# Loads ahead of the last reads, 31 tiles ahead, four last rounds by block: a hybrid retention and PEER layer on one core

## The chip, the cores and the metric

One core of a Trainium2 chip runs the whole layer. The metric is the device time of the program in microseconds (us). The engines are TensorE (PE in the profile, PEld its weight loads), VectorE (DVE), ScalarE (ACT), GpSimd (POOL) and SyncE (SP, which here only issues transfers); each works through its own instructions in order and waits on semaphores for the others. DMA transfers are issued from the queues of SP, ACT and POOL.

## The reference

512 latent tokens and 256 context tokens of width 1024, one layer, fp32. Cut to what matters here:

```python
mod = silu(c) @ ada_w + ada_b                  # six rows of 1024: sh1, sc1, g1, sh2, sc2, g2
lg = log_sigmoid(ret_decay)                    # 2 x 4 decays
proj = modulate(rmsnorm(x), sh1, sc1) @ w_in   # pooling mixer, retention q k v, gates
x = x + g1 * (merged @ w_out)                  # merged: gated sum of pooling and retention
hf = modulate(rmsnorm(x), sh2, sc2)
# PEER: 8 heads; product keys give 16 of 16384 experts to each token and head
q = hf @ wq;  s1, s2 = q . keys;  top 16 of each;  top 16 of the sums -> eidx, g = softmax
act = gelu(u[eidx] . hf)
x = x + g2 * sum over experts (g * act) * v[eidx]
out = rmsnorm(x) * final_g
```

## The kernel before

fp32 products are made of three passes (`mm3`, L151 to L153): every operand is split into a part `hi` rounded to the engine's format (`split_hi`, a cast on ScalarE) and the remainder `lo` (`split_lo`, L168, a subtraction on VectorE or, where the caller says so, GpSimd). A weight tile is loaded from DRAM into one of three `raw` buffers (`load`, L158); the buffer comes free when hi and lo have been made.

**Front.** `mods` computes the modulation vectors from 512 KB pieces of ada_w (VectorE reductions, L292) and makes the first weight groups' low parts on GpSimd. `attention` starts with 31 operations on 128x8 numbers that turn the decays into `lg`, and ends with the pooling and retention branches. `post` multiplies by w_out, adds the gated residual, normalises each block of 128 tokens (`normed`: TensorE multiplies by a diagonal matrix, which gives the transposed block, `ht` is that scaled and shifted, `hfT` its split). `row_bcast` (L199) turns one modulation vector into a tile with that vector in all 128 partitions by 16 TensorE matmuls; it is called four times, for g1, a2, s2 and, near the end, g2.

**Experts.** The tokens of block 0 take their experts one by one: 128 gathers (`fetch`, L983, a gather of u and v rows), a dot product (L991), a gelu and a combine (L1002). The other three blocks (384 tokens) take all 16384 experts densely, as 128 tiles of 128 experts: `up` (24 matmuls and a gelu) gives `a`; it is multiplied by `G`, the routing weights in dense form (`run_times`, L1145), split into ph and pl (`weigh`), and `down` adds its product with the tile's v rows into Y (18 matmuls for the three blocks).

The dense G is made in 24 rounds, the hot phase: VectorE makes one-hot matrices of 16 tokens (`onehots`), TensorE multiplies them (L1087), ScalarE moves the product into `st` (L1088), which is stored to DRAM (`gd`). G is read back in pieces of 8 tiles (`read`). In this phase up tiles are already made in halves (`run_up`), up to `AHEAD` of them, with loads `ask`ed three tiles ahead and splits made by `prep`. `tick` lets one step of the routes (`topk`) of block 0 run, interleaved with other work.

The main loop over 128 rounds j: weigh the next tile, split its v rows, load u tiles, read a part of a piece of G, `down`, dots of arrived gathers, `run_times`, combines, lows of u, up of a later tile, sometimes a tick, new gathers from round `GATHER` on. After round `LATE` the rows for the last normalisation are loaded and block 0 is finished. The last two rounds run block by block, so that each block's `finish` (scale, residual, norm, store) can start when its Y is complete.

The order on every engine is the order in which the code above is written, except where stated: no scheduler moves instructions inside the expert part, whose schedule is manual.

## Time and profile before

| | before |
|---|---|
| runs | 1816.27, 1817.89, 1818.47 us, median 1817.89 |
| profiled execution | 1820.35 us, its span 1818.6 us |
| PE busy | 1733.3 us, 95% of the span, 9913 matmuls |
| DVE / ACT / POOL busy | 1348.6 / 774.6 / 442.8 us |
| granted TensorE clock, mean | 0.988 of full speed |
| DMA | 404 MB, mean 222 GB/s |

The span is from the first to the last instruction of the profiled execution; some 1.75 us of its time lie outside it. Busy time of PE counts instructions in flight, which overlap. In a timeline row an idle time in brackets is the time for which the engine did nothing just before that instruction, with the operation whose completion ended it. A row with x2 or more joins instructions of one form that follow each other.

### The profile page before, as it was taken

To read this page: it belongs to the slowest core of one execution; us is meant where nothing else is said; L and a number is where in the kernel's file an instruction comes from. 1 tells how busy PE (TensorE), PEld (TensorE's weight loads), DVE (VectorE), ACT (ScalarE), POOL (GpSimd) and SP (SyncE) were. 2 spreads that over 40 slices of the span, in tenths; PEclk is the share of its full clock that TensorE was granted. 3 is DMA by queue.
4 is the path that set the end of the run, shared out by engine and by line. 5 is a ranking of instruction groups with operands and counts; after the bars stand their busy time and mean duration, and the time that the engine had idled before them with its cause. 6 is when DMAs were issued, how large, how long until landed. Compare 5 with 4: busy or idle time off the path is not lost.

```text
span 1818.6 us, 26049 instructions
## 1 busy us (share of the span) xinstructions
PE 1733.3 (95%) x9913; PEld 1556.5 (86%) x9913; DVE 1348.6 (74%) x2402; ACT 774.6 (43%) x1304; POOL 442.8 (24%) x403
## 2 busy tenths in 40 slices
PE   7999999999989989896999999999999999999996
PEld 4889988888989988885888888889999999999995
DVE  6866365663559999987958777887888778887766
ACT  6343245222344348872334434344444444444443
POOL 2222220001047730005622222222222222222200
PEclk9999999999999999997999999999999999999998
DMA  7311133674242226773478888889898898889852
GB/s 305 108 47 47 59 122 128 231 253 153 70 150 67 87 81 243 266 270 102 139 299 300 294 325 318 296 319 328 328 330 301 327 329 313 328 309 335 309 172 95
DMA packets 133550, 404.02 MB, mean 222 GB/s; under 512 B 10800, under 2 KB 60208, under 8 KB 113840
## 3 DMA queue, kind: packets, MB, share of 16 engines
q1 hardware_dynamic: 111104, 241.39, 39.3%
q0 software_dynamic: 18432, 134.23, 19.0%
q10 hardware_dynamic: 3888, 26.74, 3.6%
q8 instruction: 77, 1.26, 0.3%
q14 instruction: 49, 0.40, 0.1%
HBM read 372.95 MB, written 29.36 MB: 221 GB/s over the span
## 4 chain that ended last, share of the span: by engine, by line
PE 46%; DVE 7%; ACT 5%; DMA 3%; issue 2%; POOL 1%; ACTq 0%; DVEq 0%; POOLq 0%
PE Y L152 8%; PE Y L153 8%; PE Y L151 8%; PE ps L153 7%; PE ps L151 7%; PE ps L152 7%; ACT st L1088 3%; DMA raw<-uvd 2%; DVE lo L168 1%; DVE o L1075 1%; ACT hi L163 1%; DMA gd<-st 1%; DVE eq L1072 1%; DVE uv L991 1%; POOL lo L168 0%
## 5 line engine op out<-in xcount | busy, mean ns | idle before, releaser
L163 ACT CAST hi<-raw 128x1024 fp32r<-128x1024 f32 x332 | 343.6, 1050 | 232.9 <-DMA raw<-uvd 150.8
L168 DVE TENSOR_TENSOR lo<-raw,hi 128x1024 fp32r<-128x1024 f32 x285 | 364.1, 1279 | 102.7 <-ACT hi L163 100.9
L153 PE MATMUL ps<-hfT,lo 128*128 128x384 f32 x1120 | 378.5, 338 | 16.9 <-DVE lo L168 16.9
L151 PE MATMUL ps<-hfT,hi 128*128 128x384 f32 x1120 | 380.6, 340 | 8.1 <-ACT a L1110 7.6
L152 PE MATMUL ps<-hfT,hi 128*128 128x384 f32 x1120 | 376.8, 336 | 1.3 <-POOL hfT L146 1.3
L983 POOL DMA_INDIRECT uv<-uv,eidx x128 | 196.8, 1537 | 604.1 <-DVE acc L1002 572.5
L151 PE MATMUL Y<-hi,ph 128*128 128x512 f32 x768 | 301.0, 392 | 10.1 <-ACT a L1110 8.4
L152 PE MATMUL Y<-lo,ph 128*128 128x512 f32 x768 | 302.9, 394 | 6.4 <-POOL lo L168 5.8
L153 PE MATMUL Y<-hi,pl 128*128 128x512 f32 x768 | 302.6, 394 | 0.0
L153 PEld LDWEIGHTS ps<-hfT,lo 128*128 128x128 f32 x1120 | 211.3, 189 | 21.8 <-DVE lo L168 21.8
L151 PEld LDWEIGHTS ps<-hfT,hi 128*128 128x128 f32 x1120 | 211.5, 189 | 13.7 <-ACT a L1110 8.3
L152 PEld LDWEIGHTS ps<-hfT,hi 128*128 128x128 f32 x1120 | 211.6, 189 | 5.6 <-POOL hfT L146 1.8
L1002 DVE SCALAR_TENSOR_TENSOR acc<-uv,act,acc 128x1024 f32<-128x1024 f32 x127 | 163.0, 1283 | 29.1 <-ACT act L994 17.5
L151 PEld LDWEIGHTS Y<-hi,ph 128*128 128x128 f32 x768 | 145.4, 189 | 39.0 <-ACT a L1110 8.7
L152 PEld LDWEIGHTS Y<-lo,ph 128*128 128x128 f32 x768 | 145.2, 189 | 37.2 <-POOL lo L168 7.8
L1110 ACT ACTIVATE a<-ps 128x384 f32<-128x384 f32 x128 | 62.6, 491 | 259.9 <-PE ps L153 253.8
L153 PEld LDWEIGHTS Y<-hi,pl 128*128 128x128 f32 x768 | 145.1, 189 | 30.7 <-DVE pl L146 0.3
L168 POOL TENSOR_TENSOR lo<-raw,hi 128x1024 fp32r<-128x1024 f32 x47 | 119.7, 2554 | 182.5 <-ACT hi L163 182.5
L146 DVE TENSOR_TENSOR pl<-a,ph 128x384 fp32r<-128x384 f32 x128 | 73.1, 571 | 118.1 <-ACT ph L145 118.0
L991 DVE SCALAR_TENSOR_TENSOR uv<-uv,hf 128x1024 f32<-128x1024 f32 x128 | 154.4, 1219 | 0.0
L1088 ACT ACTIVATE st<-ps 128x512 f32<-128x512 f32 x96 | 91.0, 1109 | 13.2 <-DMA gd<-st 7.1
L993 ACT ACTIVATE act<-act 128x1 f32<-128x1 f32 x128 | 25.9, 202 | 162.2 <-DVE uv L991 162.2
(287 smaller groups left out, 2912.4 us busy)
## 6 DMA issues: line engine op xcount, KB each, us to landing
raw<-uvd SPq DMA_DIRECT2D x252, 512.0 KB, 6.0
ada<-ada SPq DMA_DIRECT2D x48, 512.0 KB, 5.4
gd<-st ACTq DMA_DIRECT2D x24, 1024.0 KB, 5.6
raw<-w_in SPq DMA_DIRECT2D x44, 512.0 KB, 4.2
G<-gd SPq DMA_DIRECT2D x85, 256.0 KB, 7.6
raw<-wq SPq DMA_DIRECT2D x16, 512.0 KB, 4.1
raw<-ret_out SPq DMA_DIRECT2D x8, 512.0 KB, 4.8
raw<-w_out SPq DMA_DIRECT2D x8, 512.0 KB, 3.6
```

The costliest lines, as they stand in the source:

```text
L146: (eng_lo or nc.vector).tensor_tensor(lo, src, hi.bitcast(F32), ALU.subtract)
L151: mm(out, a[0], b[0], start=first, stop=False)
L152: mm(out, a[0], b[1], start=False, stop=False)
L153: mm(out, a[1], b[0], start=False, stop=last)
L163: self.nc.scalar.copy(hi, raw)
L168: eng.tensor_tensor(lo, raw, hi.bitcast(F32), ALU.subtract)
L983: self.nc.gpsimd.indirect_dma_start(out=t, out_offset=None, in_=self.I["uv"], in_offset=bass.IndirectOffsetOnAxis(ap=self.eidx[:, s:s + 1] ...
L991: nc.vector.scalar_tensor_tensor(t[:, :D], t[:, :D], 1.0, self.hf, ALU.mult, ALU.mult, accum_out=act[:, 0:1])
L993: nc.scalar.activation(act[:, 1:2], act[:, 0:1], AF.Gelu)
L1002: nc.vector.scalar_tensor_tensor(self.acc, t[:, D:], act[:, 1:2], self.acc, ALU.mult, ALU.add)
L1088: nc.scalar.mul(st[:, :, t:t + 4].rearrange("p m t -> p t m"), ps, 1.0 / GSCALE)
L1110: nc.scalar.activation(a, ps[:, :N], AF.Gelu)
```

## The change

AHEAD 30 to 31, LATE 117 to 118, GATHER 9 to 10, and a new LAST = 4. The decay arithmetic moves out of `attention` into `decays`, called at the start of `build` with the same operations. Of the diff, cut:

```diff
+            self.md = dr.tile([4, D], F32, name="md")
...
             nc.sync.dma_start(self.cols, I["cols"])
+            self.decays(hp)
...
-                            w[g].append(self.split_w(self.load(I["w_in"][g][:, 4 * i:4 * i + 4]), nc.gpsimd))
+                            w[g].append(self.split_w(self.load(I["w_in"][g][:, 4 * i:4 * i + 4]), nc.vector))
...
+    def mod_row(self, out, v):
+
+        self.nc.sync.dma_start(out, self.md[v:v + 1].to_broadcast([P, D]))
...
         g1 = p.tile([P, D], F32, name="g1")
-        self.row_bcast(g1, self.modc[:, 0:8])
+        a2 = p.tile([P, D], F32, name="a2")
+        s2 = p.tile([P, D], F32, name="s2")
+        ps = self.ps()
+        nc.tensor.transpose(ps[0:32, 0:P], self.modc, self.ident)
+        rows = p.tile([32, P], F32, name="mrows")
+        nc.scalar.copy(rows, ps[0:32, 0:P])
+        nc.sync.dma_start(self.md.rearrange("v (k p) -> (v k) p", p=P), rows)
+        for row, v in ((g1, 0), (a2, 2), (s2, 1)):
+            self.mod_row(row, v)
...
-                    nc.vector.tensor_scalar(t[:, i], ps[:, i * P:(i + 1) * P], cols[:, 16 + k:17 + k],
-                                            cols[:, 8 + k:9 + k], ALU.mult, ALU.add)
+                    m, c = cols[:, 16 + k:17 + k], cols[:, 8 + k:9 + k]
+                    if i % 2:
+                        nc.scalar.activation(t[:, i], ps[:, i * P:(i + 1) * P], AF.Identity, scale=m, bias=c)
+                    else:
+                        nc.vector.tensor_scalar(t[:, i], ps[:, i * P:(i + 1) * P], m, c, ALU.mult, ALU.add)
                 d = [a[:, 4 * h:4 * h + 4, (b - 1) * P:b * P] for a in hT]
-                self.split(t, d[0], d[1], None, nc.gpsimd)
+                self.split(t, d[0], d[1])
...
-        a2 = p.tile([P, D], F32, name="a2")
-        s2 = p.tile([P, D], F32, name="s2")
-        self.row_bcast(a2, self.modc[:, 16:24])
-        self.row_bcast(s2, self.modc[:, 8:16])
...
-        self.run_up(4)
-        self.prep(QU + 4, nc.vector)
+        self.run_up(5)
...
-            ph = dp.tile([P, N], F32R, name="ph", tag="ph", bufs=2)
-            pl = dp.tile([P, N], F32R, name="pl", tag="pl", bufs=2)
+            if j < P - LAST:
+                ph, pl = [dp.tile([P, N], F32R, name=x, tag=x, bufs=2) for x in ("ph", "pl")]
+            else:
+                ph, pl = [self.ring.tile([P, N], F32R, name=x, tag="a", bufs=AHEAD + 1) for x in ("ph", "pl")]
...
-                self.run_up(2 if i % 3 == 2 else 1)
+                self.run_up(2 if i % 3 == 0 else 1)
...
         self.rt_es.close()
-        read(0, 18, 22)
-        read(0, 22)
+        k = self.split_to
+        self.prep(k, nc.vector)
+        self.prep(k + 1, nc.vector)
         for n in range(2):
             vs[n] = load_v(n)
         nv[1] = 2
+        read(0, 18, 22)
+        read(0, 22)
         self.dp = dp = self.pool("dense")
         place(1)
-        read(1)
-        k = len(self.acts)
-        self.prep(k + 2, nc.vector)
-        self.prep(k + 3, nc.vector)
         tick()
         tick()
         self.run_up(3)
-        self.prep(k + 4, nc.vector)
+        self.prep(k + 2, nc.vector)
...
-            run_v(min(P, j + 4 if deep else j + 2), nc.gpsimd if j + 1 < GATHER else nc.vector)
+            run_v(min(P, j + 4 if deep else j + 2), nc.vector)
...
+            if j < 2:
+                read(1, 12 * j, 12 * j + 12)
...
-            if j < P - 2:
+            if j < P - LAST:
...
+            for n in hi:
+                us[n] = self.split_lo(us[n], hi[n], nc.vector)
+                ns += 1
             for s, act in zip(ready, cr):
                 self.combine(s, slots.pop(s), act)
             done = asked[0]
-            for n in hi:
-                us[n] = self.split_lo(us[n], hi[n], nc.vector)
-                ns += 1
...
-            if j % 4 < 3:
+            if j % 10 in (0, 1, 3, 4, 6, 7, 9):
                 tick()
...
-                self.row_bcast(fin[0], self.modc[:, 24:32])
+                self.mod_row(fin[0], 3)
...
-            for j in (P - 2, P - 1):
+            for j in range(P - LAST, P):
...
-        for b in (0, 0, 1, 2, 1, 3, 1, 2, 3, 3, 2):
+        for b in (0, 0, 1, 1, 1, 2, 2, 2, 3, 3, 3):
```

The lines of the expert part are 21 higher in the changed kernel (L1145 becomes L1166).

The SyncE queue at the end of the hot phase, before. raw_8055 to raw_8262 are u tiles, G_6616 is piece 0 of G (its blocks 10 to 18, 18 to 22, 22 to 24), raw_8327 and raw_8329 are v rows of tiles 0 and 1, G_8334 is piece 1, raw_8336 the last u tile made ahead (29).

```order
L158 DMA raw_8055<-uvd 128x1024
L1124 DMA G_6616<-gd_58 128x8x128
L158 DMA raw_8187<-uvd 128x1024
L158 DMA raw_8262<-uvd 128x1024
L1124 DMA G_6616<-gd_58 128x4x128
L1124 DMA G_6616<-gd_58 128x2x128
L158 DMA raw_8327<-uvd 128x1024
L158 DMA raw_8329<-uvd 128x1024
L1124 DMA G_8334<-gd_58 128x24x128
L158 DMA raw_8336<-uvd 128x1024
```

The same place of the queue with the change: raw_8111 to raw_8318 are u tiles 27 to 30, raw_8324 and raw_8326 the v rows of tiles 0 and 1, G_6603 is piece 0 and G_8333 piece 1.

```order
L1145 DMA G_6603<-gd_59 128x8x128
L159 DMA raw_8111<-uvd 128x1024
L159 DMA raw_8193<-uvd 128x1024
L159 DMA raw_8312<-uvd 128x1024
L159 DMA raw_8318<-uvd 128x1024
L159 DMA raw_8324<-uvd 128x1024
L159 DMA raw_8326<-uvd 128x1024
L1145 DMA G_6603<-gd_59 128x4x128
L1145 DMA G_6603<-gd_59 128x2x128
L159 DMA raw_8668<-uvd 128x1024
L159 DMA raw_8674<-uvd 128x1024
L1145 DMA G_8333<-gd_59 128x12x128
```

Two u tiles and both v tiles now stand ahead of the last two reads of piece 0, and piece 1 is read in two halves further on.

VectorE where the first `a` is multiplied by G, before: the end of a tick's searches (s, sv, si), the three products, pl of tile 0, then the next step of the routes (e).

```order
L922 MATCH_REPLACE s_4759<-sv_8529,s_4759 128x128 x2
L917 MAX sv_8529<-s_4759 128x8 x2
L919 MAX_INDEX si_8530<-sv_8529,s_4759 128x8 x2
L1145 TENSOR_TENSOR a<-a,G 128x384 x3
L146 TENSOR_TENSOR pl<-a,ph 128x384
L967 TENSOR_REDUCE e_8605<-oe 128x16
```

With the change, where lo is the low part of u tile 30:

```order
L943 MATCH_REPLACE s_4732<-sv_8516,s_4732 128x128 x2
L938 MAX sv_8516<-s_4732 128x8 x2
L940 MAX_INDEX si_8517<-sv_8516,s_4732 128x8 x2
L1166 TENSOR_TENSOR a<-a,G 128x384 x3
L147 TENSOR_TENSOR pl<-a,ph 128x384
L169 TENSOR_TENSOR lo<-raw,hi 128x1024
L988 TENSOR_REDUCE e_8610<-oe 128x16
```

The ticks still stand ahead of the products, and the low part of tile 30 comes behind both.

VectorE in a round of the main loop with two gathered rows, before (lo behind pl is that of v, lo at the end that of u; L991 the dots, L1002 the combines):

```order
L146 TENSOR_TENSOR pl<-a,ph 128x384
L168 TENSOR_TENSOR lo<-raw,hi 128x1024
L991 SCALAR_TENSOR_TENSOR uv,act<-uv,hf 128x1024 x2
L1145 TENSOR_TENSOR a<-a,G 128x384
L1002 SCALAR_TENSOR_TENSOR acc<-uv,act,acc 128x1024 x2
L168 TENSOR_TENSOR lo<-raw,hi 128x1024
```

With the change (L1012 the dots, L1023 the combines):

```order
L147 TENSOR_TENSOR pl<-a,ph 128x384
L169 TENSOR_TENSOR lo<-raw,hi 128x1024
L1012 SCALAR_TENSOR_TENSOR uv,act<-uv,hf 128x1024 x2
L1166 TENSOR_TENSOR a<-a,G 128x384
L169 TENSOR_TENSOR lo<-raw,hi 128x1024
L1023 SCALAR_TENSOR_TENSOR acc<-uv,act,acc 128x1024 x2
```

The low part of u has moved ahead of the combines.

## Rows read from the trace of the kernel before

**Rows 1.** Busy time by stretch: us, busy us (instructions) by engine, PEclk, DMA share, GB/s

```profile
844.00:857.00 13.00, 11.09 (x30) 8.34 (x30) 12.43 (x43) 3.63 (x5) 9.13 (x16) 0.65 0.21 72
1150.00:1740.00 590.00, 590.00 (x2947) 532.40 (x2946) 471.37 (x583) 249.68 (x474) 140.67 (x91) 1.00 0.87 318
```

**Rows 2.** Timeline of PE: start us, us, instruction, tiles, [idle before <-releaser]

```profile
70.92 0.39 PE L151 MATMUL ps<-hi,hc 128*128 128x256 f32 x1 [2.54 <-DVE k L146]
...
507.38 0.61 PE L667 MATMUL ps<-diag,xr 128*128 128x128 f32 x4
...
518.84 0.44 PE L152 MATMUL ps<-hfT,hi 128*128 128x384 f32 x1 [1.30 <-POOL hfT L146]
...
808.12 0.33 PE L153 MATMUL ps<-hfT,lo 128*128 128x384 f32 x1
...
812.28 0.34 PE L153 MATMUL ps<-hfT,lo 128*128 128x384 f32 x1
...
828.84 0.69 PE L151 MATMUL ps<-hfT,hi 128*128 128x384 f32 x1 [7.16 <-ACT a L1110]
...
843.59 0.79 PE L151 MATMUL Y<-hi,ph 128*128 128x512 f32 x1 [8.42 <-ACT a L1110]
...
873.76 0.50 PE L152 MATMUL Y<-lo,ph 128*128 128x512 f32 x1 [1.82 <-POOL lo L168]
...
884.14 0.50 PE L152 MATMUL Y<-lo,ph 128*128 128x512 f32 x1 [1.81 <-POOL lo L168]
...
1027.41 0.44 PE L153 MATMUL ps<-hfT,lo 128*128 128x384 f32 x1 [1.13 <-DVE lo L168]
...
1748.59 1.95 PE L199 MATMUL ps<-ident,modc 128*128 128x128 f32 x16
...
1789.46 0.50 PE L151 MATMUL Y<-hi,ph 128*128 128x512 f32 x1 [1.71 <-ACT ph L145]
...
1805.87 0.39 PE L153 MATMUL Y<-hi,pl 128*128 128x512 f32 x1
```

**Rows 3.** Timeline of DVE in the front

```profile
22.43 1.22 DVE L292 SCALAR_TENSOR_TENSOR junk<-ada,crow 128x1024 f32<-128x1024 f32 x1
...
24.05 2.90 DVE L292 SCALAR_TENSOR_TENSOR junk<-ada,crow 128x1024 f32<-128x1024 f32 x1 [0.39 <-DMA ada<-ada]
```

**Rows 4.** Timeline of POOL: the normed blocks, and the first rounds

```profile
516.49 4.54 POOL L146 TENSOR_TENSOR hfT<-ht,hfT 128x512 fp32r<-128x512 f32 x2 [2.70 <-ACT hfT L145]
...
850.25 2.67 POOL L168 TENSOR_TENSOR lo<-raw,hi 128x1024 fp32r<-128x1024 f32 x1
```

**Rows 5.** Timeline of DVE in the hot phase

```profile
689.22 1.22 DVE L1072 TENSOR_TENSOR eq<-ioh,ig 128x2048 f16<-128x2048 f16 x1
...
693.76 1.22 DVE L168 TENSOR_TENSOR lo<-raw,hi 128x1024 fp32r<-128x1024 f32 x1
```

**Rows 6.** Timeline of SP's queue at the end of the hot phase

```profile
804.50 9.97 SPq L1124 DMA_DIRECT2D G<-gd  x2
...
816.47 20.76 SPq L158 DMA_DIRECT2D raw<-uvd  x3
```

**Rows 7.** Timeline of ACT at the last tile made ahead

```profile
827.35 1.04 ACT L163 CAST hi<-raw 128x1024 fp32r<-128x1024 f32 x1 [13.94 <-DMA raw<-uvd]
```

**Rows 8.** Timeline of DVE from the last low parts on, and its last passes

```profile
814.01 0.48 DVE L917 MAX8 sv<-s 128x8 f32<-128x128 f32 x2
...
818.49 0.29 DVE L919 FIND_INDEX8 si<-sv,s 128x8 uint32<-128x128 f32 x1
...
829.57 0.21 DVE L917 MAX8 bv<-cs 128x8 f32<-128x54 f32 x1
...
841.69 1.47 DVE L1145 TENSOR_TENSOR a<-a,G 128x384 f32<-128x384 f32 x3
...
850.62 3.38 DVE L168 TENSOR_TENSOR lo<-raw,hi 128x1024 fp32r<-128x1024 f32 x1
...
1812.59 2.74 DVE L1019 SCALAR_TENSOR_TENSOR od<-od,ss,uv 128x512 f32<-128x512 f32 x4
```

More of the change, by code (lines that the diff above doesn't have):

```diff
@@ L39 @@
 NH = 2
-AHEAD = 30
+AHEAD = 31
 JE = 121
-LATE = 117
-GATHER = 9
+LATE = 118
+LAST = 4
+GATHER = 10
 LAG = 2
@@ L240, in front, with decays @@
                 self.post(op, hx, ys)
+    def decays(self, hp):
+        nc, I = self.nc, self.I
+        dc = hp.tile([P, 8], F32, name="dc")
+        nc.sync.dma_start(dc, I["decay"].to_broadcast([P, 8]))
+        e = hp.tile([P, 8], F32, name="lg_e")
+        z = hp.tile([P, 8], F32, name="lg_z")
+        z2 = hp.tile([P, 8], F32, name="lg_z2")
+        lg = hp.tile([P, 8], F32, name="lg")
+        nc.vector.tensor_scalar(e, dc, -1.0, None, ALU.mult)
+        nc.vector.tensor_tensor(e, e, dc, ALU.min)
+        nc.scalar.activation(e, e, AF.Exp)
+        nc.vector.tensor_scalar(z, e, 2.0, None, ALU.add)
+        nc.vector.reciprocal(z, z)
+        nc.vector.tensor_tensor(z, z, e, ALU.mult)
+        nc.vector.tensor_tensor(z2, z, z, ALU.mult)
+        nc.vector.memset(e, 1.0 / 19)
+        for i in range(17, 0, -2):
+            nc.vector.tensor_tensor(e, e, z2, ALU.mult)
+            nc.vector.tensor_scalar(e, e, 1.0 / i, None, ALU.add)
+        nc.vector.tensor_tensor(e, e, z, ALU.mult)
+        nc.vector.tensor_scalar(z, dc, 0.0, None, ALU.min)
+        nc.vector.scalar_tensor_tensor(lg, e, -2.0, z, ALU.mult, ALU.add)
+        nlb = hp.tile([P, 4], F32, name="nlb")
+        nc.vector.tensor_scalar(nlb, lg[:, 4:8], -1.0, None, ALU.mult)
+        lc = hp.tile([P, 8], F32, name="lc")
+        nc.vector.tensor_scalar(lc[:, 0:4], lg[:, 0:4], 256.0, None, ALU.mult)
+        nc.vector.tensor_scalar(lc[:, 4:8], lg[:, 4:8], 512.0, None, ALU.mult)
+        self.lg = lg, nlb, lc
     def mods(self, hx, hcx):
@@ L395, in attention @@
         nc.sync.dma_start(rel, I["kc"][:, K_REL:K_REL + 1536])
-        dc = ap.tile([P, 8], F32, name="dc")
-        nc.sync.dma_start(dc, I["decay"].to_broadcast([P, 8]))
-        e = ap.tile([P, 8], F32, name="lg_e")
-        z = ap.tile([P, 8], F32, name="lg_z")
-        z2 = ap.tile([P, 8], F32, name="lg_z2")
-        lg = ap.tile([P, 8], F32, name="lg")
-        nc.vector.tensor_scalar(e, dc, -1.0, None, ALU.mult)
-        nc.vector.tensor_tensor(e, e, dc, ALU.min)
-        nc.scalar.activation(e, e, AF.Exp)
-        nc.vector.tensor_scalar(z, e, 2.0, None, ALU.add)
-        nc.vector.reciprocal(z, z)
-        nc.vector.tensor_tensor(z, z, e, ALU.mult)
-        nc.vector.tensor_tensor(z2, z, z, ALU.mult)
-        nc.vector.memset(e, 1.0 / 19)
-        for i in range(17, 0, -2):
-            nc.vector.tensor_tensor(e, e, z2, ALU.mult)
-            nc.vector.tensor_scalar(e, e, 1.0 / i, None, ALU.add)
-        nc.vector.tensor_tensor(e, e, z, ALU.mult)
-        nc.vector.tensor_scalar(z, dc, 0.0, None, ALU.min)
-        nc.vector.scalar_tensor_tensor(lg, e, -2.0, z, ALU.mult, ALU.add)
-        nlb = ap.tile([P, 4], F32, name="nlb")
-        nc.vector.tensor_scalar(nlb, lg[:, 4:8], -1.0, None, ALU.mult)
-        lc = ap.tile([P, 8], F32, name="lc")
-        nc.vector.tensor_scalar(lc[:, 0:4], lg[:, 0:4], 256.0, None, ALU.mult)
-        nc.vector.tensor_scalar(lc[:, 4:8], lg[:, 4:8], 512.0, None, ALU.mult)
+        lg, nlb, lc = self.lg
         def pair(shape, name, bufs=1):
@@ L727, in queries @@
         s0 = tp.tile([P, PH, 1, 2, P], F32, name="s0")
-        self.acts, self.us, self.uraw, self.ul = [], {}, {}, QU
+        self.acts, self.us, self.uraw = [], {}, {}
+        self.ul = self.split_to = QU
         with tc.manual_schedule():
@@ L882, in prep @@
     def prep(self, n, eng):
-        if n < AHEAD and n not in self.us:
+        if self.split_to <= n < AHEAD:
             self.ask(n + 3)
             self.us[n] = self.split_w(self.uraw.pop(n), eng)
+            self.split_to = n + 1
     def ups(self):
```

## The prediction

> **What bounds the kernel now.** I read the busy time by stretches first, then TensorE's timeline for its idle gaps, then for each gap the timeline of the engine that ended it. Over the 590 us of the main loop TensorE is busy for all 590 at full clock, VectorE for 471 and the DMA engines for 87% [rows 1]; there only fewer or shorter TensorE instructions could gain, and the change takes none out of the 128 rounds. A round is 18 matmuls of the down projection: 71 steps between the first and the last of the last four rounds take 16.41 us, 0.231 each with the gaps at its start, so 4.1 us for 18. An up tile is 24 matmuls: from one matmul to the one 24 later 4.16 us [rows 2]. What can be won lies in the gaps outside that stretch. The profiled execution took 1820.35 us, the span 1818.6 of it and 1.75 around it; the median of the runs is 1817.89, 2.46 less. I add the gains against the profiled execution and take the 2.46 off at the end.
>
> **The change part by part.**
>
> *Front.* While GpSimd makes low parts, VectorE's 128x1024 reduction goes from 1.22 to 2.90 us [rows 3]; four of them are stretched so. Moving these low parts to VectorE costs 1.2 us each and takes the stretch away: about even, and under the ada loads anyway. The 31 tiny decay instructions now stand at the program's start, where VectorE's first work waits for a load. Before, they stood among those that make k, and TensorE waited 2.54 us for k [rows 2], then about 3 us more in two smaller gaps. I take 4 us of the 5.5. Bounds: 0, if the rotary tables, whose loads are now behind one weight tile, are late instead; 6, if all goes.
>
> *Row broadcasts.* Each of the four calls is 16 matmuls, 1.95 us [rows 2]. The first and the last stand in otherwise full stretches, and become one transpose, and one DMA read issued long before use: 1.7 + 1.9 = 3.6. Bounds 2 and 3.7. The SyncE queue now holds the write of the four rows and three reads; the first read waits for the write's landing, and one w_out load is queued behind it. The first consumer of g1 then comes some 5 us later than before, but six PSUM buffers of 2.8 us each lie in between, so TensorE doesn't see it.
>
> *Last normed block.* From the first of its matmuls at 507.38 to the query projection's second matmul at 518.84 TensorE alternates this block's matmuls with those of two broadcasts and waits for VectorE's ht; its last wait, 1.30 us, is for GpSimd's low parts of the block [rows 2], two in 4.54 us [rows 4]. After: no broadcast matmuls, half of ht on ScalarE, the low parts on VectorE. Counting VectorE's list with uncontended durations (two ts, recip, hf of 1.28, low parts of 0.7) the query starts near 514.4 and doesn't stop: 4.4 us. Bounds 2 and 6. The Trainium skill, page ScalarE: Activation LUTs, section Table sets, says that identity is in every table set, so no table is loaded for it; no run here shows that for identity yet, and a load for each half would leave 1.8 of the 4.4 by the estimate from the 1.28 us load that this trace shows for Sqrt.
>
> *Hot phase (24 rounds).* VectorE is the bound: four one-hot passes from 689.22 to 693.76, 4.54 us, then a low part of 1.2 in two of three rounds [rows 5]. The tile halves move from i%3=2 to i%3=0, with the same low parts; one low part more is made ahead. Nothing gained in a round; the fifth half before the softmax fills a wait of TensorE for the gate weights, which lets the phase end 0.6 to 2 us sooner (in the next term).
>
> *End of the phase, to the first down matmul.* Here lies the biggest gap. Before, SyncE issues the reads of G for blocks 18 to 22 and 22 to 24 at 804.50 and is held 9.97 us, until the last store has landed; v0, v1, a whole piece of G and then the load of the last tile follow, that one at 816.47 [rows 6]. Its raw data is there at 827.35 [rows 7], TensorE restarts at 828.84 after 7.16 us, and again waits 8.42 us until 843.59 [rows 2], because a(0) stands on VectorE behind the top-k ticks, from 829.57 to 841.69 [rows 8]. After, the loads of tiles 29 and 30 and of v0 and v1 stand ahead of the G reads, and piece 1 of G comes later in halves. So tile 29 is there while VectorE makes low parts 27 and 28 (end about 809.7). Then two ticks as before (814.01 to 818.8, 4.8 us), lo(29) of 1.2: 815.7. Then VectorE has the same list of 12.1 us to a(0) as from 829.57 before [rows 8]: a(0) at 827.8. TensorE has run out at 820.8 after tiles 26 to 29. Its next tile, 30, is new; its hi on ScalarE stands behind ph(0), which needs a(0), and its lo on VectorE behind a and pl: hi near 829.4, lo 831. After such gaps the granted clock falls: 0.65 over the stretch from 844 [rows 1]. At that, tile 30 takes 4.16 / 0.65 = 6.4 us from 831, ends at 837.4, and the first down matmul starts near 838.2 instead of 843.59, with one tile (4.2) more done: 5.4 + 4.2 = 9.6. Bounds: 4, if lo(30) or G is later; 24, if VectorE's list no longer decides.
>
> *First rounds of the loop.* In rounds with a tick the waits of TensorE for GpSimd's lo repeat 10.38 us apart (873.76, 884.14) [rows 2] while its own work is 4.1 + 4.2 = 8.3. VectorE's lo takes 3.38 beside GpSimd's lo of 2.67, and 1.2 alone [rows 4, 5, 8]. After, both lo's are VectorE's, 2.4 together: 9.4 in a tick round, and ticks come in 7 of 10 rounds instead of 3 of 4, so the mean falls below 8.3. Three waits of about 1.9 and their small fellows go: 6. The granted clock of 0.65 from 844 to 857 [rows 1], with 30 matmuls in 11.1 us of busy time, gives back perhaps 2: 8 in all. Bounds 3 and 11. The burst of gathers, one round later, I set at nothing (-2 to +4); it hides as before behind the acts already made.
>
> *Order in the loop.* In rounds with two dots TensorE waits 1.13 us for lo(u) [rows 2], four times in all, the last at 1143.51, since two combines of 1.3 stand ahead of it. Lo ahead of combine takes these away: 4.5. Bounds 3 and 5; elsewhere TensorE is at pace and gains nothing. VectorE has 590 - 471 = 119 us of slack here for the wait that lo(u) may now have for its hi.
>
> *Tail.* Blocks come 24 matmuls (5.5 us) apart instead of 12, so VectorE keeps up with the finish of each, and only one block is left after the last matmul, near 8 us for it instead of the 12.3 from 1806.26 to 1818.6 [rows 2]: VectorE's last four scale passes from 1812.59 [rows 8] become two. Against it: block 0 needs ph of 125 only 6 matmuls (1.4 us) after that of 124, with f0's finish in between on VectorE and ScalarE; the 1.71 us wait at 1789.46 [rows 2] grows by 4.1 - 1.4 = 2.7. Net 4.3 - 2.7 = 1.6, I take 1. Bounds -2 and 5.
>
> Sum: 4 + 3.6 + 4.4 + 9.6 + 8 + 4.5 + 1 = 35.1. 1820.35 - 35.1 - 2.46 = 1782.8.
>
> **Rivals.**
> A, *VectorE's list shortens too*: with no piece-1 read and no lo beside it a(0) comes 12 us earlier, and the gap at 821 closes almost. For: GpSimd's lo of v0 lies inside that list. Against: that lo still is GpSimd's, and the ticks, whose chain runs over GpSimd, are the same. Gain 14 more: 1769. The Trainium skill, page Trainium Kernel Development and Optimization, section Key Constraints, says that all queues share the same 16 DMA engines; v0 and v1, 1 MB now ahead of G, would then set G back by 3.3 us at the 318 GB/s of the loop's row, and in this rival, where G decides, leave 1772.
> B, *the waits move on*: VectorE, with more low parts in rounds 0 to 9 and in the front, ends the waits instead of GpSimd, and the tail's stall eats its gain. For: it is busy 12.4 of the 13 us from 844 to 857 [rows 1]. Against: the stretch by GpSimd's lo goes. Front 1, broadcasts 3.6, normed 2, phase end 4, rounds 3, order 4.5, tail -1: 17, so 1801.
> C, *the other side*: lo(u) ahead of combine makes VectorE, in program order, wait in every round for ScalarE's hi and so for a late raw load, with the next pl behind it. VectorE's slack is 119 us over about 79 rounds of 7.5 us, 1.5 a round; to eat 35 us more over some 110 rounds takes 0.3 a round, so from about 1.8 us of added wait in each round it decides, and the time would be over 1818; at 2.2 it is 1827. Against: in the two-dot rounds lo(u) came late for the combines ahead of it, not for its hi, and lo earlier frees its raw buffer earlier.
> D, *it doesn't do what it says*: each raw load waits for one of three raw buffers, and if tile 29's still came after the last store, 9.6 would go, 1793; to reach no change the front and rounds must give nothing too.
>
> **How the numbers follow.** The forecast as summed 0.60 (own range 1775 to 1791, from the bounds of the two biggest terms taken half), A 0.11, B with D's part 0.21, no change at all 0.03, C 0.05. Measuring can tell about 0.2%, 3.6 us, from no change: faster 0.92, same 0.03, slower 0.05. The range reaches to A and B: 1768 to 1802; about 0.15 lies outside.
>
> **What would show it.** Right: no L199 matmul after the front; the raw load of tile 29 issued before the G reads; first down matmul near 838 with 31 tiles done and one gap of 8 to 10 us from about 821; no waits for a GpSimd lo after 850; none of 1.13 at the two-dot rounds; about 8 us from the last matmul to the end. Wrong: a(0) much before or after 828; first rounds still over 9 us apart; a new wait for rp or k in the front; VectorE waiting for hi in every round of the loop.

## The result and the profile after

The changed kernel takes 1790.07 us, the median of four runs (1790.03 to 1790.19). The kernel before took 1817.78 beside it (1816.27 to 1818.47, four runs). The ratio is 0.9848, with a 95% interval of 0.9834 to 0.9862: 27.7 us faster, where the forecast had 34.8. The profiled execution of after took 1790.08 us, its span 1788.3. Against the span of before, 1818.6, that is 30.3 us; 2.5 of it is that the profiled execution of before took that much more than the median of its runs, and the table below holds them too.

To see where the 30.3 us came from, I took the start of the same matmul in both traces at ten places. An up tile that one kernel has done more by then counts 4.16 us, its time in [rows 2].

| place | gain so far, us | the stretch gave | forecast |
|---|---|---|---|
| 114 us, end of the front | 2.4 | 2.4 | 4 |
| last matmul by w_out | 1.65 | -0.8 | 1.7 (first broadcast) |
| first matmul of the keys | 2.4 | 0.7 | 4.4 (last normed block) |
| first down matmul | 7.8 | 5.4 | 9.6 |
| round 12 | 18.3 | 10.5 | 8 |
| round 14 | 22.95 | 4.7 | 0 (gathers) |
| round 40 | 28.5 | 5.6 | 4.5 (order) |
| round 121 | 30.4 | 1.9 | 1.9 (last broadcast) |
| last matmul | 27.15 | -3.25 | |
| end | 30.3 | 3.1 | with the row above: 1 (tail) |

The first down matmul starts at 839.98 instead of 843.59, with one tile more done, hence 3.61 + 4.16 = 7.77 in its row. The sum is near the forecast, but it is made of other parts. Each row is one execution; how far such rows differ between kernels with the same code there is said ahead of the experiments. Now the rows that answer to those of before.

Part 1 of the page after, busy us (share of the span) and instructions by engine. TensorE keeps its work and its share rises:

```profile
PE 1725.9 (97%) x9850; PEld 1551.5 (87%) x9850; DVE 1333.1 (75%) x2408; ACT 774.9 (43%) x1310; POOL 358.9 (20%) x385
```

Busy time by stretch, after (columns as in [rows 1]):

```profile
505.00:513.00 8.00, 5.09 (x24) 3.79 (x22) 7.50 (x12) 4.22 (x9) 5.03 (x2) 0.76 0.74 280
513.00:520.00 7.00, 6.47 (x20) 6.07 (x21) 2.49 (x4) 1.42 (x3) 0.00 (x0) 0.54 0.66 250
823.50:833.00 9.50, 0.52 (x3) 0.27 (x2) 7.12 (x28) 2.16 (x4) 6.45 (x14) 0.67 0.17 56
833.00:840.00 7.00, 6.17 (x25) 5.34 (x25) 6.69 (x30) 0.64 (x3) 3.94 (x12) 0.72 0.24 77
840.00:857.00 17.00, 17.00 (x81) 14.82 (x82) 15.71 (x50) 6.90 (x10) 7.36 (x19) 1.00 0.56 165
1150.00:1740.00 590.00, 590.00 (x2944) 532.09 (x2944) 468.05 (x582) 246.19 (x472) 105.66 (x88) 1.00 0.89 314
```

The first rounds now run with TensorE full at a granted clock of 1.00 (840 to 857, where [rows 1] had 0.65 from 844 to 857). The main loop is as full as before. In exchange there is a stretch at 0.54 that was not there: the query projection from 513.

TensorE's timeline after, which answers to [rows 2]:

```profile
72.85 0.58 PE L152 MATMUL ps<-hi,hc 128*128 128x256 f32 x1 [2.81 <-DVE k L147]
...
457.90 0.38 PE L152 MATMUL ps<-hi,mg 128*128 128x256 f32 x1 [0.30 <-ACT mg L146]
458.93 0.38 PE L154 MATMUL ps<-hi,mg 128*128 128x256 f32 x1 [0.53 <-DVE mg L147]
...
513.50 0.69 PE L152 MATMUL ps<-hfT,hi 128*128 128x384 f32 x1 [0.77 <-ACT hfT L146]
...
810.08 0.44 PE L152 MATMUL ps<-hfT,hi 128*128 128x384 f32 x1 [1.50 <-ACT hi L164]
...
832.73 0.69 PE L152 MATMUL ps<-hfT,hi 128*128 128x384 f32 x1 [8.98 <-ACT hi L164]
...
839.98 0.50 PE L152 MATMUL Y<-hi,ph 128*128 128x512 f32 x1 [0.58 <-ACT a L1131]
...
1761.88 0.80 PE L152 MATMUL Y<-hi,ph 128*128 128x512 f32 x1 [3.13 <-ACT ph L146]
...
1778.71 0.40 PE L154 MATMUL Y<-hi,pl 128*128 128x512 f32 x1
```

Two gaps of 7.16 and 8.42 us became one of 8.98. There is still a wait for k at the front, 2.81 us, and the tail has a wait of 3.13 us in place of 1.71.

VectorE's timeline after, in the front, at the end of the hot phase and in the tail ([rows 8] before):

```profile
69.16 0.69 DVE L470 TENSOR_SCALAR tabt<-rel,nlb 128x896 f32<-128x896 f32 x1 [5.85 <-issue]
...
810.06 2.36 DVE L169 TENSOR_TENSOR lo<-raw,hi 128x1024 fp32r<-128x1024 f32 x2 [7.87 <-ACT hi L164]
...
817.02 1.21 DVE L169 TENSOR_TENSOR lo<-raw,hi 128x1024 fp32r<-128x1024 f32 x1
818.14 0.21 DVE L938 MAX8 bv<-cs 128x8 f32<-128x54 f32 x1
...
830.27 1.47 DVE L1166 TENSOR_TENSOR a<-a,G 128x384 f32<-128x384 f32 x3
...
832.71 1.22 DVE L169 TENSOR_TENSOR lo<-raw,hi 128x1024 fp32r<-128x1024 f32 x1 [0.50 <-ACT hi L164]
```

From the merge of the top-k (bv) to a(0) VectorE needs 830.27 - 818.14 = 12.13 us, as from 829.57 to 841.69 in [rows 8]. But the list starts 2.4 us later than I had it: VectorE was idle for 7.87 us ahead of 810.06, for a hi on ScalarE, with two ticks of top-k still to come behind that low part. On ScalarE that hi stands behind the last four copies into st, which end at 808.53.

The 12.13 us are not all work of VectorE. In them it waits 1.78 us for GpSimd (oe), which makes the low part of v0 just before that; the list of before has the same wait:

```profile
827.29 0.63 DVE L974 TENSOR_TENSOR oh<-ioh,pos 128x896 f16<-128x896 f16 x1 [1.78 <-POOL oe L983]
```

```profile
823.11 2.35 POOL L169 TENSOR_TENSOR lo<-raw,hi 128x1024 fp32r<-128x1024 f32 x1
825.42 1.83 POOL L983 TENSOR_TENSOR oe<-oh,ci 128x864 f32<-128x864 f16 x1
```

SyncE's queue and ScalarE after, at the same place ([rows 6, 7]). The four loads are those of tiles 29 and 30 and of v0 and v1, and the reads of G now stand behind them. Tile 29 is there when ScalarE comes to its hi at 811.26, without a wait, where before it was made at 827.35:

```profile
802.22 16.36 SPq L159 DMA_DIRECT2D raw<-uvd  x4
818.67 0.94 SPq L1145 DMA_DIRECT2D G<-gd  x2
```

```profile
804.81 3.72 ACT L1109 ACTIVATE st<-ps 128x512 f32<-128x512 f32 x4
...
808.98 2.00 ACT L164 CAST hi<-raw 128x1024 fp32r<-128x1024 f32 x2 [0.45 <-ACT st L1109]
...
811.26 1.04 ACT L164 CAST hi<-raw 128x1024 fp32r<-128x1024 f32 x1
...
830.84 0.51 ACT L146 CAST ph<-a 128x384 fp32r<-128x384 f32 x1 [12.74 <-DVE a L1166]
831.64 1.03 ACT L164 CAST hi<-raw 128x1024 fp32r<-128x1024 f32 x1
```

TensorE's waits from 840 to 1740, us in total, times, longest. Those for GpSimd's low parts, of which [rows 2] has two, are gone; these two are all:

```profile
PE Y L153 <- DVE lo L169: 0.6, 2, 0.5
PE Y L152 <- ACT a L1131: 0.6, 1, 0.6
```

### The profile page after: what moved, and what is told of

Same layout as the page of the kernel before. It is cut to its first block, busy times and chain, and to the rows that moved or that the text cites. A ratio compares the mean times of both kernels' runs of the same rounds, so it can differ in the third digit from the quotient of the medians.

```text
span 1788.3 us, 25956 instructions
## 1 busy us (share of the span) xinstructions
PE 1725.9 (97%) x9850; PEld 1551.5 (87%) x9850; DVE 1333.1 (75%) x2408; ACT 774.9 (43%) x1310; POOL 358.9 (20%) x385
## 4 chain that ended last, share of the span: by engine, by line
PE 50%; DVE 5%; ACT 4%; issue 1%; DMA 1%; POOL 0%; ACTq 0%; DVEq 0%; POOLq 0%
PE Y L153 9%; PE Y L154 9%; PE Y L152 9%; PE ps L154 8%; PE ps L152 8%; PE ps L153 8%; ACT st L1109 3%; DVE o L1096 1%; DVE lo L169 1%; DMA gd<-st 1%; DVE eq L1093 1%; ACT hi L164 0%; DVE si L940 0%; DMA raw<-uvd 0%; PE ps L1108 0%
## 5 line engine op out<-in xcount | busy, mean ns | idle before, releaser
L1004 POOL DMA_INDIRECT uv<-uv,eidx x128 | 153.8, 1201 | 639.3 <-DVE acc L1023 601.5
L1023 DVE SCALAR_TENSOR_TENSOR acc<-uv,act,acc 128x1024 f32<-128x1024 f32 x127 | 162.5, 1279 | 5.0
L1012 DVE SCALAR_TENSOR_TENSOR uv<-uv,hf 128x1024 f32<-128x1024 f32 x128 | 154.4, 1218 | 0.0
L169 POOL TENSOR_TENSOR lo<-raw,hi 128x1024 fp32r<-128x1024 f32 x35 | 85.6, 2456 | 241.4 <-ACT hi L164 241.4
L152 PE MATMUL ps<-hx,hi 128*128 128x512 f32 x224 | 88.2, 394 | 1.1 <-ACT yTt L597 1.1
```

Of the source, the lines that this page charges most:

```text
L152: mm(out, a[0], b[0], start=first, stop=False)
L169: eng.tensor_tensor(lo, raw, hi.bitcast(F32), ALU.subtract)
L1004: self.nc.gpsimd.indirect_dma_start(out=t, out_offset=None, in_=self.I["uv"], in_offset=bass.IndirectOffsetOnAxis(ap=self.eidx[:, s:s + 1] ...
L1012: nc.vector.scalar_tensor_tensor(t[:, :D], t[:, :D], 1.0, self.hf, ALU.mult, ALU.mult, accum_out=act[:, 0:1])
L1023: nc.vector.scalar_tensor_tensor(self.acc, t[:, D:], act[:, 1:2], self.acc, ALU.mult, ALU.add)
```

## The experiments

All are edits of the changed kernel, and each ratio is against the kernel before, measured beside it; the changed kernel's is 0.9848. "Gains" are against the trace of before, as in the table. Each kernel has one trace, so I compare stretches first and totals second, and a stretch can be judged by the kernels that have the same code there. Their gains:

| stretch | gain of the kernels with the same code there, us |
|---|---|
| start to 114 us | 0.7 to 4.1 |
| from there to the last matmul by w_out | -0.2 to 0.3, the changed kernel -0.8 |
| from there to the keys | 0.5 to 1.9 |
| last matmul of the hot phase to the first down matmul | 4.5 to 5.8, and 6.6 in the one kernel whose hot phase took longer |
| first down matmul to round 12 | 9.8 to 10.5 |
| round 20 to 40 | 5.6 in each |
| round 121 to the end | -0.5 to 0.4 |

One trace does not show a difference that is smaller than these spreads.

### Two rounds at the end again

```
-LAST = 4
+LAST = 2
-        for b in (0, 0, 1, 1, 1, 2, 2, 2, 3, 3, 3):
+        for b in (0, 0, 1, 2, 1, 3, 1, 2, 3, 3, 2):
```

> The changed kernel with two last rounds by block instead of four, and the old order of the finishes. My theory: the four rounds gave nothing, since the 3.1 us won behind the last matmul were paid by a wait for ph of round 125 that grew to 3.3 us in block 0; so 1790 again, within 1 us, the first wait back near 1.9 us and the stretch from the last matmul to the end back near 12.3. Rival: the longer wait has another cause (f0 one round later), the four rounds gave some 3 us and the time rises to 1793.

1787.94 us, ratio 0.9821 [0.9799, 0.9842]. From round 117 to the end it gains 3.5 us, the changed kernel 1.7. The wait of block 0, in TensorE's timeline of this kernel, is 0.35 us instead of 3.13:

```profile
1762.44 0.50 PE L152 MATMUL Y<-hi,ph 128*128 128x512 f32 x1 [0.35 <-ACT ph L146]
```

Neither theory had it: four rounds block by block cost 1.8 us against two. Behind the longer wait the changed kernel's granted clock falls too, which its busy time shows (columns as in [rows 1]):

```profile
1762.00:1767.00 5.00, 5.00 (x15) 4.02 (x16) 3.73 (x9) 3.19 (x5) 0.00 (x0) 0.67 0.02 3
```

From 1761.88 it takes 3.5 us for eight matmuls that take 1.9 at full clock. With two rounds the clock stays at 1.00 over the same stretch.

### Low part of u behind the combines again

```
-            for n in hi:
-                us[n] = self.split_lo(us[n], hi[n], nc.vector)
-                ns += 1
             for s, act in zip(ready, cr):
...
             done = asked[0]
+            for n in hi:
+                us[n] = self.split_lo(us[n], hi[n], nc.vector)
+                ns += 1
```

> The changed kernel with the low part of u behind the combines again. My theory: four waits of 1.1 to 1.3 us of TensorE in the rounds with two dots come back, 5.6 us by the difference of the traces: 1795.5. Rival: with GATHER at 10 and fewer ticks VectorE is early anyway and the order gave nothing: 1790.

1788.32 us, ratio 0.9831 [0.9806, 0.9855]. Between rounds 20 and 40 it gains the same 5.6 us (25.2 to 30.75), and no wait for the low part of an up tile came back. All waits of TensorE in this kernel from 900 to 1760:

```profile
PE Y L152 <- ACT ph L146: 3.2, 1, 3.2
PE Y L153 <- DVE lo L169: 0.5, 1, 0.5
```

My theory, that the order took the waits away, falls. The two later runs on the phase of the rounds, below, show what did.

### GpSimd makes the low parts of v in rounds 0 to 9 again

```
-            run_v(min(P, j + 4 if deep else j + 2), nc.vector)
+            run_v(min(P, j + 4 if deep else j + 2), nc.gpsimd if j + 1 < GATHER else nc.vector)
```

> The changed kernel with the low parts of v of rounds 0 to 9 on GpSimd again; the ticks stay in 7 of 10 rounds. My theory: VectorE's low part goes back from 1.2 to 3.4 us beside GpSimd's, and in the rounds with a tick TensorE waits again: of the 11.3 us won in rounds 0 to 12 some 6 go, 1796. Rival A: the rarer ticks alone gave it, 1791. Rival B: the full clock behind the first down matmul gave it and the low parts nothing, 1790.

1795.46 us, ratio 0.9863 [0.984, 0.9887]. From the first down matmul to round 12 it gains 3.3 us instead of 10.5. The stretched low part is back on VectorE, in its timeline here, and so is the wait, in those of TensorE from 840 to 1740:

```profile
850.45 3.38 DVE L169 TENSOR_TENSOR lo<-raw,hi 128x1024 fp32r<-128x1024 f32 x1
```

```profile
PE Y L153 <- POOL lo L169: 5.2, 3, 2.0
```

So the home of the low parts is worth 7.2 us, and all the rest 3.3. The two kernels part only behind round 2: up to there both gain 6.7 us, and from round 2 to 12 the changed kernel gains 3.8 while this one loses 3.4. What the first two rounds had lost before stands in TensorE's timeline of before: one wait of 1.91 us, and 24 matmuls that start some 0.43 us apart instead of 0.23, 4.7 us in all:

```profile
844.18 0.63 PE L152 MATMUL Y<-lo,ph 128*128 128x512 f32 x1
844.61 0.63 PE L153 MATMUL Y<-hi,pl 128*128 128x512 f32 x1
...
852.97 0.62 PE L152 MATMUL Y<-lo,ph 128*128 128x512 f32 x1 [1.91 <-POOL lo L168]
```

### Reads of G ahead of the loads

```
         self.rt_es.close()
+        read(0, 18, 22)
+        read(0, 22)
...
         nv[1] = 2
-        read(0, 18, 22)
-        read(0, 22)
...
         place(1)
+        read(1)
...
-            if j < 2:
-                read(1, 12 * j, 12 * j + 12)
```

> The changed kernel with the reads of the last blocks of G, the loads of v0 and v1 and the whole piece 1 in the order of before, ahead of the splits of tiles 27 and 28; the loads that these splits ask for (29, 30) come behind them. My theory: tile 29 is late again, by the landing of a store, two reads and piece 1; a(0) then comes 8 to 10 us later and with it the first down matmul: 1796 to 1799. Rival: only VectorE's list of 12.1 us counts, which starts with the low part of tile 29 either way but could run ahead of it: 1791.

1789.79 us, ratio 0.9831 [0.981, 0.9853]. From the end of the hot phase to the first down matmul it gains 3.4 us instead of 5.8. SyncE's queue is held 9.85 us again; a(0) on VectorE comes at 831.99 instead of 830.27:

```profile
802.94 9.85 SPq L1145 DMA_DIRECT2D G<-gd  x2
```

```profile
831.99 1.47 DVE L1166 TENSOR_TENSOR a<-a,G 128x384 f32<-128x384 f32 x3
```

The order on the queue is worth 2.4 us against the changed kernel's trace, and 1.1 against the lowest with the same code; the medians of the runs, 1789.79 and 1790.07, don't show it. Either is less than the 6 to 9 of my theory. The whole piece of G still stood behind the load of tile 29 here, so only part of the edit was undone.

### All but the last broadcast on TensorE again

```
-        for row, v in ((g1, 0), (a2, 2), (s2, 1)):
-            self.mod_row(row, v)
+        self.row_bcast(g1, self.modc[:, 0:8])
...
+        self.row_bcast(a2, self.modc[:, 16:24])
+        self.row_bcast(s2, self.modc[:, 8:16])
```

> The changed kernel with g1, a2 and s2 by TensorE matmuls again, at their old places (48 more matmuls); g2 stays a DMA read. My theory: TensorE has nothing else to do there. At g1 the 1.7 us of matmuls cover the wait for mg that took their place; at the query projection they keep TensorE's clock at 2.4 GHz, so that its matmuls step 0.173 from the start instead of 0.320 us for 17 of them. The query's last matmul then ends within 0.7 us of the changed kernel's, and the time is 1790 to 1791. Rival: the matmuls are real work and cost 1.7 + 3.4 us, the low clock has another cause and stays: 1795.

1790.59 us, ratio 0.985 [0.9833, 0.9866]: level, with 48 matmuls more. Busy time by stretch of this kernel, to hold beside that of after:

```profile
505.00:513.00 8.00, 6.03 (x51) 5.64 (x51) 7.06 (x11) 4.98 (x12) 5.04 (x2) 1.00 0.73 283
513.00:520.00 7.00, 6.52 (x37) 6.07 (x37) 2.84 (x4) 2.42 (x6) 0.00 (x0) 1.00 0.60 212
```

The granted clock stays at 1.00 and 37 matmuls fit where 20 did. From the last matmul by w_out to the keys the gain is 2.7 us instead of 0.7. The changed kernel's trace is near the lower end here: in the eleven kernels without these two broadcasts the granted clock over the 7 us that begin 0.5 us ahead of the first query matmul lies between 0.50 and 0.72, and the gain between 0.5 and 1.9; the two kernels with them have 1.00 and 2.7. So they are worth 0.7 to 2.2 us. At the first broadcast the gain is -0.2, which is level with the kernels that read g1 by DMA. The total shows none of it, since this kernel's hot phase took 130.3 us instead of 127.2. I can't explain that; in the last kernel below, which has two of these broadcasts too, it wasn't so.

### Tile 30 ahead of a(0) on VectorE

```
         self.prep(k + 2, nc.vector)
+        self.prep(k + 3, nc.vector)
         tick()
```

> The changed kernel with the split of u tile 30 right behind that of tile 29, ahead of the last two ticks. My theory: TensorE's wait of 9 us for hi of tile 30 goes, since this hi stands behind ph(0) on ScalarE only by program order; the wait moves to the first down matmul, which needs a(0) behind VectorE's ticks, at 832.5 instead of 840, so 7 us less: 1783. Rival: the low part ahead of the ticks sets a(0) back by 1.2 us and the half clock stays, so 1787 to 1790.

1788.88 us, ratio 0.9839. From the hot phase's end to the first down matmul it gains 4.9 us, within the 4.5 to 5.8 of the kernels without the edit: nothing won. In TensorE's timeline of this kernel the wait only has another releaser:

```profile
831.34 0.69 PE L152 MATMUL ps<-hfT,hi 128*128 128x384 f32 x1 [7.61 <-ACT a L1131]
```

The inputs were there, but tile 30 waited for a PSUM buffer, whose gelu stands on ScalarE behind ph(0), and so behind a(0).

### a(0) ahead of the last two ticks

```
+        self.prep(k + 3, nc.vector)
         tick()
         self.run_up(2)
-        run_v(1, nc.gpsimd)
-        tick()
+        run_v(1, nc.vector)
...
         self.run_up(2 * AHEAD)
+        tick()
```

> As the run before, and the products and splits of tile 0 ahead of the fourth tick, the low part of v0 on VectorE. My theory: a(0) waits for nothing but the last read of G, which lands at 823.3, so the first down matmul follows the up tiles almost at once, near 828, at full clock: 11 to 12 us less than the changed kernel, 1778 to 1779. Rival: the tick that now comes later pushes the routes past round 9, or the reads of G land later under more transfers, and half of that is given back: 1784.

1787.67 us, ratio 0.9832. The first down matmul starts at 833.28, a gain of 12.8 us instead of 5.8. Two rounds later it is 13.0 against 12.5: TensorE now waits there for a low part on VectorE, which has the tick that was put off to do:

```profile
833.28 0.50 PE L152 MATMUL Y<-hi,ph 128*128 128x512 f32 x1 [0.58 <-ACT a L1131]
...
841.28 0.79 PE L153 MATMUL Y<-lo,ph 128*128 128x512 f32 x1 [3.40 <-DVE lo L169]
```

VectorE's whole list up to about round 2 decides, and its order does not.

### Gathers one round earlier, ticks in three of four rounds

```
-GATHER = 10
+GATHER = 9
-            if j % 10 in (0, 1, 3, 4, 6, 7, 9):
+            if j % 4 < 3:
```

> The changed kernel with the gathers from round 9 and a tick in three of four rounds, as before. My theory: the 3.9 us that the trace shows as won between rounds 10 and 14 come from the gathers' burst meeting fewer late loads one round later, and are lost again, with 0 to 2 us in the first rounds: 1794 to 1796. Rival: it was the earlier progress of the up tiles that covered the burst: 1790 to 1791.

1791.96 us, ratio 0.9863 [0.9844, 0.9883]. From the first down matmul to round 14 it gains 13.1 us instead of 15.2, and from 20 to 40 still 5.6. The two numbers carry 2.1 of the 15.2: 1.8 between rounds 12 and 14, and only 0.3 up to round 12. With the low parts on VectorE the rarer ticks thus hardly count there.

### The phase of the rounds, with the low part ahead and behind

```
-            return min(P, AHEAD + (j + 1) * (P - AHEAD) // JE)
+            return min(P, AHEAD + max(0, j - 1) * (P - AHEAD) // JE)
```

In every fifth round no up tile is made, and in every fifth two gathered rows are combined instead of one. This edit puts both into the same rounds. The second kernel has the low part behind the combines too, as two experiments above.

> The changed kernel with the rounds that make no up tile moved by two, so that the 20 rounds with two gathered rows (17, 22, ...) are those without an up tile, as four of them were before; the low part of u stays ahead of the combines. Both theories: no wait, 1790 to 1792 (a tile less ahead in the last rounds). If waits come all the same, the order ahead of the combines is no protection.

> The same shift of the rounds, with the low part of u behind the combines. My theory now, after the order alone turned out to cost nothing: the four waits of before came where a round has two gathered rows and no up tile, so that TensorE needs the low part 4.2 us sooner; with 97 tiles over 121 rounds such rounds no longer meet. Forced to meet, some 20 rounds wait 1.3 to 1.4 us: 26 us more than the run before, 1815 to 1818. Rival: the waits went because VectorE is ahead since GATHER is 10, and this kernel takes what the run before takes.

With the low part ahead: 1794.78 us, ratio 0.9872, and no wait for a low part of u in the loop. From the first down matmul to round 12 it gains 5.2 us, the changed kernel 10.5: the edit leaves rounds 1 and 2 without an up tile, and in rounds 2 and 3 TensorE waits 2.16 and 2.24 us for a low part of v. The first of the two, in its timeline here:

```profile
849.35 0.65 PE L153 MATMUL Y<-lo,ph 128*128 128x512 f32 x1 [2.16 <-DVE lo L169]
```

With it behind: 1822.14 us, ratio 1.0021 [1.0011, 1.003]. All waits of TensorE in that kernel from 900 to 1780:

```profile
PE ps L154 <- DVE lo L169: 23.8, 21, 1.1
```

That is 27.4 us between the two, and it needs both: a round with two combines and no up tile to cover them, and the low part behind them.

### Two ticks first, and the table of distances loaded earlier

```
+            nc.sync.dma_start(self.rel, I["kc"][:, K_REL:K_REL + 1536])
             project(0)
...
-        nc.sync.dma_start(rel, I["kc"][:, K_REL:K_REL + 1536])
...
         self.rt_es.close()
+        tick()
+        tick()
...
         place(1)
-        tick()
-        tick()
```

> The changed kernel with two edits in different stretches. First, the two ticks ahead of the splits of tiles 27 and 28, where VectorE idles 7.9 us for ScalarE: a(0) 4.8 us earlier, and since VectorE's work from there to round 3 is what decides, the gain stays: 4 to 5 us at the fifth round. Rival: it is given back in the first rounds as in the run with tile 0 weighed earlier: 0 to 1. Second, the table of differences loaded before the last two weight tiles of the front: the 2.8 us wait for k falls to about 1, 1.5 to 2.5 us. Together 1783 to 1785; by the rivals 1788 to 1790.

1780.90 us, ratio 0.9796 [0.9779, 0.9812]. At 114 us the gain is 8.05 instead of 2.4, and TensorE no longer waits for k: VectorE has the table of distances (rel) at 62.13 instead of 69.16. From the end of the hot phase to the first down matmul it gains 9.45 instead of 5.8, and that stays through the rounds. VectorE's timeline of this kernel:

```profile
62.13 0.69 DVE L471 TENSOR_SCALAR tabt<-rel,nlb 128x896 f32<-128x896 f32 x1
...
803.14 3.50 DVE L169 TENSOR_TENSOR lo<-raw,hi 128x1024 fp32r<-128x1024 f32 x3 [3.46 <-ACT hi L164]
...
819.68 1.47 DVE L1167 TENSOR_TENSOR a<-a,G 128x384 f32<-128x384 f32 x3
```

The ticks now fill half of the idle stretch ahead of the low parts (3.46 us left of 7.87). Against the kernels with the same code, the edit of rel wins 4 to 7 us at 114 us, and the ticks 3.6 to 5; in the last kernel below the ticks win 1.7 to 3.

### What was found, in one kernel

The kernel above, with two rounds at the end, and with the broadcasts of a2 and s2 on TensorE again.

> The run before with two more edits: two last rounds by block with the old order of finishes, and a2 and s2 by TensorE matmuls at their old place (g1 and g2 stay DMA reads). My theory: the tail gives 1.8 us, as in the run with two last rounds, and the matmuls keep the clock up at the query projection for 1.9 more, so 1777 to 1778. Rival: the hot phase takes 3 us longer whenever the broadcasts are matmuls, as in the run with all three of them, and eats both: 1780 to 1782.

1777.69 us in five runs (1776.94 to 1778.85), ratio 0.9775 [0.9762, 0.9788]. By the medians that is 0.7% less than the changed kernel. The tail gives 2.1 us more than in the kernel above and the query projection 1.4. Against it, the stretch from the hot phase's end to the first down matmul gains 7.5 us instead of 9.45. The query projection's first two matmuls take 0.45 and 0.44 us, where those of after take 0.69. TensorE's timeline of this kernel:

```profile
507.15 0.45 PE L152 MATMUL ps<-hfT,hi 128*128 128x384 f32 x1 [0.20 <-ACT hfT L146]
507.87 0.44 PE L153 MATMUL ps<-hfT,hi 128*128 128x384 f32 x1 [0.28 <-DVE hfT L147]
...
1751.55 0.50 PE L152 MATMUL Y<-hi,ph 128*128 128x512 f32 x1 [0.42 <-ACT ph L146]
```

## Why the prediction was nearly right, point by point

**Front, 4 forecast, 2.4 measured.** The term fell short near the lower bound's reason: a table was late instead, not a rotary one but rel, which VectorE needs first. VectorE stands idle for 5.85 us until it reads rel at 69.16, and loading rel earlier takes the wait for k away. Moving the decay instructions alone left it: 2.81 us, 2.54 before.

**Row broadcasts.** The last gave its 1.9. The step "so TensorE doesn't see it" failed for the first: g1 itself isn't waited for, but with the 1.95 us of matmuls gone TensorE meets mg's splits, in waits of 0.30 and 0.53 us, and the broadcast restored costs nothing (-0.2 us, where the kernels without it have -0.8 to 0.3). What had been hidden beside those matmuls was ScalarE's and VectorE's work on mg.

**Last normed block.** The step "and doesn't stop: 4.4" failed. The first query matmul came 3.6 us earlier (517.12 to 513.50), but TensorE had had waits and few matmuls ahead of it, and from 513 to 520 the granted clock was 0.54, near its lower level of 1.2 GHz; from 518.8 to 525 before, it was 1.00. With the matmuls of a2 and s2 back it is 1.00 again. The Trainium skill, page TensorE: Matmul & The Clock Gate, section Part 1, says that the throttled rate is the default and that activity releases it. The trace agrees: 24 matmuls in the 8 us ahead without the broadcasts and 0.54 behind them, 51 with the broadcasts and 1.00. The other step, that ScalarE's half of ht needs no table load, was right: between 508.75 and 514.46 ScalarE's timeline has no load, and its 128x128 pieces of ht take 0.46 us.

**Hot phase's end, 9.6 forecast, 5.4 measured.** The mechanism was right: one gap of 9 us, a(0) on VectorE, a list of 12.1 us, tile 30 behind ph(0). The term was mis-sized by its start: the low parts of tiles 27 and 28 ended at 812.4 and not at 809.7, so a(0) came at 830.27 and not at 827.8. By the table's count it is 4.9 us late, since the kernel was 2.4 us ahead at the keys. Of this 1 to 2.4 us are that the fifth half tile ahead of the softmax did not let the phase end 0.6 to 2 us sooner: from the keys to its last matmul 0.4 us were lost. What remains is of the size that filling VectorE's wait for a hi behind ScalarE's copies won: 3.6 us in the run with the ticks first, 1.7 in the last kernel. The forecast had no term for that wait, though the trace of before has it too, ahead of its last low parts:

```profile
811.73 2.36 DVE L168 TENSOR_TENSOR lo<-raw,hi 128x1024 fp32r<-128x1024 f32 x2 [3.96 <-ACT hi L163]
```

Rival A, a shorter list, did not come, and neither did D: tile 29's load was issued ahead of the reads of G. The runs with tile 30 ahead and with a(0) ahead gave less than 1 us that stayed to round 12; work put into VectorE's idle time gave 1.7 to 5. That the 1.78 us for GpSimd inside the list could go with v0's low part on VectorE was not tried by itself.

**First rounds, 8 forecast, 10.5 measured.** Right in the mechanism: 7.2 by the home of the low parts, 3.3 by the rest. The clock was mis-sized, "perhaps 2" where the rows of before show 4.7 us. Rival B, VectorE ending the waits in GpSimd's place, did not come: from 840 to 1740 two are left, 0.6 us in all. VectorE's low part takes 3.38 us beside GpSimd's, 1.22 alone. The Trainium skill, page SBUF — State Buffer, section Who interferes with whom, says that a VectorE instruction with two SBUF inputs contends with a GpSimd one that reads SBUF. The trace agrees, with 3.38 against 1.22 us.

**Gathers, nothing forecast, 4.7 measured.** The bound of +4 was the nearer end. 1.8 us go back to GATHER and the tick rule; the other 2.9 I have not separated.

**Order in the loop, 4.5 forecast, 5.6 measured.** Right in size, and wrong in its cause: "Lo ahead of combine takes these away" is the step that failed. With the low part behind the combines the 5.6 us came all the same. What took the waits away is that 97 up tiles over 121 rounds, from 31 tiles ahead, leave the rounds without an up tile at 0, 5, 10 and so on, away from those with two combines (17, 22, 27). Before, 98 tiles made the two meet in rounds 21, 26, 31 and 36: four waits. Moved by two rounds they meet in every fifth round, and then the order does matter: 21 waits, 27.4 us. The edit of the order is an insurance that this setting doesn't need. Rival C, VectorE held by hi in every round, did not come: from 1150 to 1740 VectorE waits 49 times for a hi, 19.3 us in all and 0.5 at most; before, it was 51 times, 31.2 us and up to 3.0.

**Tail, +1 forecast, -0.1 measured.** Both halves were there: 9.6 us from the last matmul to the end (1788.3 - 1778.71) instead of 12.7, and a wait of 3.13 us for ph. The end gave 3.1 us and the wait took 1.4, 3.13 instead of 1.71. What the forecast left out is the clock behind that wait, 0.67 from 1762 to 1767, some 1.6 us. Two rounds at the end, with a wait of 0.35, are better by 1.8 us.

The forecast of 1783 was 7 us below 1790. The terms make 4.8 of it: too much by 4.2 at the hot phase's end, 3.7 in the normed block, 4.1 in the broadcast and the front and 1.1 in the tail, too little by 8.3 in first rounds, gathers and order; that these balance so far was luck, and the front and the normed block, in other kernels with the same code there, come out anywhere from 0.7 to 4.1 and from 0.5 to 1.9. The other 2.5 is the excess of the profiled execution of before, which I took off beside the sum while the measured gains hold it.

## What to carry to other kernels

When a gap ends at one engine's list, sum that list from the engine's last idle stretch to the first round where the others catch up, and fill its idle time before reordering it; here two ticks moved forward won what two reorderings did not. Where two periodic kinds of work share an engine, write down in which rounds they fall: a change of one start number can decide whether the code's order matters at all. Before taking out work that fills gaps on TensorE, or making a wait longer, look at what it will wait for next, and at the granted clock of the dense stretch behind it. And before reading a difference of 1 us off one trace, look at what the same code took in others.

## What the runs showed of the hardware that was not expected

The 32 small matmuls of two broadcasts, in among the waits ahead of the query projection, went with a granted clock of 1.00 over that projection; without them it was 0.54, and 0.50 to 0.72 in the eleven kernels with the same code there; the first 128x384 matmul took 0.69 us instead of 0.45. In the last kernel tile 30 took 8.1 us, from 820.95 to the wait of 0.58 ahead of 829.63, and 6.4 in the kernel without the two broadcasts (822.13 to the same wait ahead of 829.12), though the code there is the same; which clock a stretch behind a gap gets was not settled. Nor was the hot phase that took 3 us longer in one kernel.
